# Reordered merge rounds in a hybrid decoder layer: sums and lower parts apart from their casts, weights loaded three units ahead

## The chip, the cores and the metric

The kernel runs on one core of a Trainium2 chip. The core has five engines that run side by side, each through its own list of instructions in a fixed order, and that meet only through semaphores: TensorE (PE in the profile, its weight loads PEld), VectorE (DVE), ScalarE (ACT), GpSimd (POOL) and SyncE (SP), whose list here is mainly the DMA queue that all large loads stand in. The metric is the device time of one execution in microseconds (us), as the median of several runs.

## The reference

One decoder layer over 1024 tokens and a model width of 1024, in float32. A state-space mixer and a latent attention run in parallel from the same projection; this case concerns what joins them.

```python
y_ssd = ssd_mixer(...) @ w_ssd_proj[i]          # (1024 x 2048) @ (2048 x 1024)
y_mla = mla_mixer(...) @ w_mla_proj[i]
g_ssd, g_mla = jnp.split(jax.nn.sigmoid(gates + gate_b[i]), 2, axis=-1)
x = x + (g_ssd * y_ssd + g_mla * y_mla) @ w_o[i]
h = rms_norm(x, norm_ffn_g[i])
u = causal_depthwise_conv(h @ w_up[i], conv_ffn_w[i], conv_ffn_b[i])
u_gate, u_val = jnp.split(u, 2, axis=-1)
x = x + (jax.nn.silu(u_gate) * u_val) @ w_down[i]
```

## The kernel before

Every float32 matmul is done as three matmuls of two-part numbers: an operand is split into a high part, which ScalarE casts (`S.copy`), and a low part, which VectorE (or GpSimd) makes as the operand less its high part; `mm3` multiplies high by high, high by low and low by high. So each operand costs a cast and a subtraction, and the subtraction waits for the cast. `split`, `ordered_split` and `quarter_split` do this (lines L146 and L153 are the casts, L148 and L154 the low parts).

The *merge* is the product of the state-space output with `w_ssd_proj`. It is cut in two along the tokens, along the inner dimension and along the outputs, and the eight products of quarters are got from seven (a Winograd scheme). Products 1 and 2 take quarters as they are; 7, 6, 5, 3 and 4 take sums and differences of activations, of weights or of both. Product p has four tiles of 128 outputs, i = 0 to 3, so there are 28 *units* (p, i), numbered 0 to 27 in the order 1, 2, 7, 6, 5, 3, 4. A unit is eight steps of three 128x128x512 matmuls. Units 0 and 1 are done by `first_products` ahead of the merge; units 2 to 27 are the loop `for n in range(2, len(units))`.

Inside unit n the loop prepares what comes next: it loads the weights of unit n+2 (`weights_raw`), sums and splits those of unit n+1 (`weights`), and sums and splits two tiles of activations for the next product (`acts`), whose raw values were loaded a unit before (`acts_raw`). Weights' sums are kept in `e1`, activations' sums in `sums` (both tiles called `x2` in the trace, or `x`). Each activation goes through sum, cast, low part before the next one starts. After its matmuls, `finish_unit` copies the bank (ScalarE) or adds it (VectorE). In products 3 and 4 the gates come in: `gates` loads two tiles of 256 KB (`gt` from `g_d`, the gate, `mt` from `m_d`, the attention's share), `gated` makes two VectorE operations of them and a finished bank, and `merged` splits the result for the next stage (one ScalarE pass, one VectorE operation).

The weights' high and low parts (`whi`, `wlo`) have two buffers each, `wraw` two, `lt` three. `ur1` and `ur2` are two buffers each of 512 KB.

The *w_o stage* follows: for each half of the tokens and each half of the outputs (`ch`), four steps of 24 matmuls, each with 512 KB of `w_o` loaded into two `wraw` tiles and split, with the remaining gates in between. At the end of four steps the banks are added to the residual `x`, which has been loaded into a tile of 2 MB for each half. In the second half `w_up` is split for the feed-forward stage (`w_raw` loads it into `ur1` and `ur2`).

At the end, the kernel ties the instructions of each engine, SP's DMAs among them, to the order of the program text for the range from `merge` to `merge_end`; outside it TensorE alone is tied throughout, and the other engines are placed by a scheduler, which may set an untied instruction between tied ones.

## Time and profile before

| | |
|---|---|
| median of 3 runs | 2222.56 us (2220.64 to 2222.77) |
| the profiled execution | 2221.28 us, span 2219.5 us |
| TensorE busy | 2136.7 us, 96% of the span |
| VectorE, ScalarE, GpSimd busy | 1501.0, 1074.4, 868.2 us |
| mean granted clock of TensorE | 0.992 |
| the loop of the merge (units 2 to 27) in the trace | from 1266 to 1469.5 us |
| the first half of the w_o stage | from 1469.5 to 1513 us |

Time in a trace is counted from the start of the span. A matmul's busy time overlaps with the next one's, so TensorE's pace is read from starts, not from busy time. In the rows of chains and waits an arrow points back at what was waited for: `PE dps L175 <- ACT whi L153` is TensorE at line 175, which waits for ScalarE's write of `whi` at line 153.

### The profile page before, as it was taken

To read this page: it belongs to the slowest core of one execution; us is meant where nothing else is said; L and a number is where in the kernel's file an instruction comes from. 1 tells how busy PE (TensorE), PEld (TensorE's weight loads), DVE (VectorE), ACT (ScalarE), POOL (GpSimd) and SP (SyncE) were. 2 spreads that over 40 slices of the span, in tenths; PEclk is the share of its full clock that TensorE was granted. 3 is DMA by queue.
4 is the path that set the end of the run, shared out by engine and by line. 5 is a ranking of instruction groups with operands and counts; after the bars stand their busy time and mean duration, and the time that the engine had idled before them with its cause. 6 is when DMAs were issued, how large, how long until landed. Compare 5 with 4: busy or idle time off the path is not lost.

```text
span 2219.5 us, 30213 instructions
## 1 busy us (share of the span) xinstructions
PE 2136.7 (96%) x10748; PEld 1696.6 (76%) x10748; DVE 1501.0 (68%) x2637; ACT 1074.4 (48%) x2044; POOL 868.2 (39%) x969
## 2 busy tenths in 40 slices
PE   8999999999999999999999988699999999999999
PEld 7877777777777887778878765577778888888887
DVE  4466656676673479898877656566886667667873
ACT  5445454545454446565654433234665455554431
POOL 2234433443343246665555200001178777750000
PEclk9999999999999999999999999899999999999999
DMA  4221111111113224545276564665133233338852
GB/s 146 72 64 54 40 48 59 54 40 47 65 44 116 73 95 136 197 143 180 91 249 197 185 209 137 221 202 180 48 114 105 100 109 104 105 136 307 281 192 81
DMA packets 129143, 278.93 MB, mean 126 GB/s; under 512 B 14112, under 2 KB 26336, under 8 KB 128992
## 3 DMA queue, kind: packets, MB, share of 16 engines
q1 hardware_dynamic: 115536, 232.82, 31.3%
q0 software_dynamic: 11968, 40.90, 5.4%
q10 hardware_dynamic: 1488, 3.28, 0.4%
q8 instruction: 84, 1.38, 0.3%
q14 instruction: 67, 0.55, 0.1%
HBM read 210.36 MB, written 66.58 MB: 125 GB/s over the span
## 4 chain that ended last, share of the span: by engine, by line
PE 66%; DVE 17%; ACT 6%; DMA 6%; issue 3%; POOL 1%; SPq 0%; ACTq 0%; DVEq 0%; POOLq 0%
PE lin L175 11%; PE lin L177 11%; PE lin L176 11%; PE dps L177 6%; PE dps L175 6%; PE dps L176 6%; PE pv L694 2%; PE s L175 2%; DVE xg L836 2%; PE s L176 2%; PE s L177 2%; DVE wlo L154 1%; PE s L651 1%; DMA gt<-g_d 1%; ACT whi L153 1%
## 5 line engine op out<-in xcount | busy, mean ns | idle before, releaser
L175 PE MATMUL lin<-h,whi 128*128 128x512 f32 x1248 | 518.0, 415 | 5.9 <-ACT whi L153 3.8
L177 PE MATMUL lin<-h,wlo 128*128 128x512 f32 x1248 | 489.5, 392 | 2.1 <-DVE wlo L154 2.1
L176 PE MATMUL lin<-h,whi 128*128 128x512 f32 x1248 | 488.1, 391 | 0.0
L175 PEld LDWEIGHTS lin<-h,whi 128*128 128x128 f32 x1248 | 234.9, 188 | 82.7 <-issue 33.8
L177 PEld LDWEIGHTS lin<-h,wlo 128*128 128x128 f32 x1248 | 234.4, 188 | 55.9 <-DVE wlo L154 4.0
L176 PEld LDWEIGHTS lin<-h,whi 128*128 128x128 f32 x1248 | 235.6, 189 | 45.8 <-issue 7.0
L154 POOL TENSOR_TENSOR wlo<-wraw,whi 128x512 fp32r<-128x512 f32 x134 | 192.4, 1453 | 173.3 <-ACT whi L153 169.5
L153 ACT CAST whi<-wraw 128x512 fp32r<-128x512 f32 x192 | 116.1, 619 | 173.6 <-PE lin L176 74.1
L688 POOL TENSOR_TENSOR acc<-acc,e 128x512 f32<-128x512 f32 (+3 forms) x80 | 78.8, 985 | 245.2 <-ACT e L683 223.3
L683 ACT ACTIVATE e<-s 128x512 f32<-128x512 f32 (+1 forms) x192 | 93.4, 492 | 152.2 <-DVE s L681 131.1
L175 PE MATMUL dps<-h,whi 128*128 128x512 f32 x244 | 101.1, 414 | 27.9 <-ACT whi L153 27.9
L1163 DVE TENSOR_TENSOR xlo<-ur,xhi 128x512 fp32r<-128x512 f32 (+1 forms) x40 | 82.8, 2071 | 58.6 <-ACT xhi L1162 58.6
L1171 POOL TENSOR_TENSOR us<-ur 128x512 f32<-128x512 f32 x20 | 29.9, 1497 | 203.0 <-DMA ur<-in_w_up 201.6
L177 PE MATMUL dps<-h,wlo 128*128 128x512 f32 x244 | 101.3, 415 | 6.8 <-DVE wlo L154 6.8
L874 ACT ACTIVATE seg<-abc,acum 128x128 f32<-128x128 f32 x256 | 80.2, 389 | 48.8 <-PE yp L915 41.9
L176 PE MATMUL dps<-h,whi 128*128 128x512 f32 x244 | 99.3, 407 | 0.0
L175 PE MATMUL dps<-tq,h 128*128 128x512 f32 x242 | 95.6, 395 | 0.0
L176 PE MATMUL dps<-tq,h 128*128 128x512 f32 x242 | 95.5, 394 | 0.0
L177 PE MATMUL dps<-tq,h 128*128 128x512 f32 x242 | 95.5, 394 | 0.0
L836 DVE SCALAR_TENSOR_TENSOR xg<-craw,cl,xg 128x1024 f32<-128x1024 f32 x48 | 73.7, 1536 | 27.4 <-ACT xg L834 26.9
L175 PEld LDWEIGHTS dps<-h,whi 128*128 128x128 f32 x244 | 48.8, 200 | 43.1 <-ACT whi L153 33.7
L688 DVE TENSOR_TENSOR acc<-acc,e 128x512 f32<-128x512 f32 (+3 forms) x80 | 55.0, 688 | 37.9 <-ACT e L683 37.3
(673 smaller groups left out, 5403.2 us busy)
## 6 DMA issues: line engine op xcount, KB each, us to landing
wraw<-in_w_main SPq DMA_DIRECT2D x112, 256.0 KB
ur<-in_w_up SPq DMA_DIRECT2D x43, 512.0 KB
abc<-ac_d POOLq DMA_DIRECT2D x32, 512.0 KB, 5.2
ar<-f_d SPq DMA_DIRECT2D x32, 512.0 KB
lt<-y_d SPq DMA_DIRECT2D x47, 256.0 KB
g_d<-lt SPq DMA_DIRECT2D x32, 256.0 KB
z_d<-lt SPq DMA_DIRECT2D x32, 256.0 KB
zt<-z_d POOLq DMA_DIRECT2D x32, 256.0 KB, 3.3
```

The source lines that it names most:

```text
L153: S.copy(hi, raw)
L154: (eng or V).tensor_sub(lo, raw, hi.bitcast(F32))
L175: PE.matmul(ps, lhsT=ah, rhs=bh, start=first, stop=False, **more)
L176: PE.matmul(ps, lhsT=ah, rhs=bl, start=False, stop=False, **more)
L177: PE.matmul(ps, lhsT=al, rhs=bh, start=False, stop=last, **more)
L683: S.activation(e[:, c0:512], ps[:, 0:w], AF.Exp)
L688: (V if hd else G).tensor_tensor(accs[hd][:, c0:512], accs[hd][:, c0:512], e[:, c0:512], op=ALU.add)
L694: PE.matmul(pv[hd * 64:(hd + 1) * 64, c0:512], lhsT=vt[:, j, hd * 64:(hd + 1) * 64], rhs=es[hd][:, c0:512], start=first, stop=last)
L836: V.scalar_tensor_tensor(c, raw[:, k:k + T], col(cw + k), c, op0=ALU.mult, op1=ALU.add)
L874: S.activation(seg[:, hd, :], abc[:, hd, :], AF.Relu, bias=acum[:, c, 8 * g + hd:8 * g + hd + 1], scale=-1.0)
L1163: eng.tensor_sub(lo, r, hi.bitcast(F32))
L1171: eng.tensor_tensor(q.s[:, 0:4, :], q.r2[:, 0:4, :], q.r2[:, 4:8, :], op=ALU.add)
```

## The change

It rewrites the merge loop's order and some loads around it.

- `acts` is cut in three: `acts_sum` (VectorE), `acts` (two casts), `acts_low` (two low parts). A unit runs both sums, then both casts, then the close of the unit before, then both low parts.
- `weights` is cut in two: `weights_sum(n + 2)`, and `weights(n + 1)` with cast and low part. `weights_raw` is called for unit n+3 instead of n+2. All units but 2 load their weights into `ur1` and `ur2`; every second activation tile goes to `wraw` instead of `lt`.
- The four tiles of `e1`, loaded at once ahead of the loop before, are loaded one in each of units 2 to 5. `e1` and `sums` change places in memory.
- `finish_unit` of a unit is called in the next one. The gate work of products 3 and 4 (`gate_first`, `gate_second`) now lies wholly within the loop; two of its eight were in the w_o stage.
- Gates' loads are placed by a table (`loads`, `pairs_of`): those of gates 0, 1 and 2 in products 6 and 5, the others one to three units ahead of use.
- The residual of each half is loaded in four pieces of 512 KB, the first half's in units 24 to 27, the second's in the first four steps of w_o. The weights of w_o's first two steps are loaded in units 25 and 27, those of the first step split in unit 27. The loads of `w_up` are tied to stand behind what SP has issued by then.

The core of the diff:

```diff
-            e1, e2 = [ep.tile([P, 4, D], F32, name="x2") for _ in range(2)]
+            e2, e1 = [ep.tile([P, 4, D], F32, name="x2") for _ in range(2)]
             sums = e2.rearrange("p i (k c) -> p (i k) c", c=512)
...
             def weights_raw(n):
                 if n < len(units):
                     p, i = units[n]
-                    if p in plain:
-                        raws[n] = quarter_raw(plain[p][0] + i, plain[p][1])
+                    ct, h = plain.get(p) or other[p]
+                    if n == 2:
+                        raws[n] = quarter_raw(ct + i, h)
                     else:
                         raws[n] = up.tile([P, KD, P], F32, name=f"ur{1 + n % 2}", bufs=2).rearrange(flat)
-                        raw_q(raws[n], other[p][0] + i, other[p][1])
-
-            def weights(n):
+                        raw_q(raws[n], ct + i, h)
+
+            def weights_sum(n):
...
-                    ws[n] = quarter_split(r if p in plain else [r if p < 6 else e])
+
+            def weights(n):
+                if n == len(units):
+                    ws[n] = wo_split(0, 0, wo_first)
+                    wo_first.extend(wo_raw(0, 1))
+                else:
+                    r = raws[n]
+                    ws[n] = quarter_split(r if n == 2 else [e1[:, units[n][1]] if units[n][0] in (7, 6) else r])
 
             def acts_raw(m):
-                if m < len(sources):
+                if 0 <= m < len(sources):
                     p, kk = sources[m]
                     h, half = {7: (0, 1), 6: (1, 1), 5: (0, 0), 3: (1, 0), 4: (1, 1)}[p]
-                    fresh[m] = raw_load(y_d, quarter_k(kk, h), hs_(half), lt.tile([P, 512], F32, name="lt"))
+                    t = wpool.tile([P, 512], F32, name="wraw", bufs=2) if m % 2 else lt.tile([P, 512], F32, name="lt")
+                    fresh[m] = raw_load(y_d, quarter_k(kk, h), hs_(half), t)
                     if p == 7:
                         raw_load(y_d, quarter_k(kk, 0), hs_(0), sums[:, kk])
 
...
-                forms[p].append(ordered_split(r if p > 5 else t))
+            def acts_sum(m):
+                if 0 <= m < len(sources):
...
+
+            def acts(ms):
+                ms = [m for m in ms if 0 <= m < len(sources)]
+                new = []
+                for m in ms:
+                    p, kk = sources[m]
+                    r, t = sums[:, kk] if p > 5 else fresh[m], act_tile()
+                    S.copy(t[:, 0, :], r)
+                    forms[p].append(t)
+                    new.append((r, t))
+                return new
+
+            def acts_low(new):
+                for r, t in new:
+                    V.tensor_sub(t[:, 1, :], r, t[:, 0, :].bitcast(F32))
+
+            def gates_raw(i, one):
+
+                if i not in gm:
+                    if i in (2, 6):
+                        u = up.tile([P, KD, P], F32, name="us", bufs=1).rearrange(flat)
+                        gm[i] = u[:, 0:512], u[:, 512:1024]
+                    else:
+                        gm[i] = [em.tile([P, 512], F32, name=n) for n in ("gt", "mt")]
+                nc.sync.dma_start(out=gm[i][one], in_=(m_d if one else g_d)[i * P:(i + 1) * P, hs_(0)])
...
-            def second_quadrant(i, gm):
-                ml.append(merged(gated(gm, X[i], mr[i]), act_tile()))
-
-            for i in range(2):
-                finish_unit(1, i)
-            weights_raw(2)
+            def gate_first(i):
+                ma.append(merged(gated(gm[i], us[i][:, 0, :], us[i][:, 0, :]),
+                                 em.tile([P, 2, 512], F32R, name="ma", bufs=4)))
+
+            def gate_second(i):
+                ml.append(merged(gated(gm[4 + i], X[i], mr[i]), act_tile()))
...
+            bigs = []
+
+            def x_load(half, i):
+                r0 = half * 512 + i * P
+                nc.sync.dma_start(out=bigs[half][:, i], in_=x[r0:r0 + P, :])
+
+            loads = {(6, 0): (0, 0), (6, 1): (0, 1), (6, 2): (1, 0), (6, 3): (1, 1), (5, 0): (2, 0), (5, 1): (2, 1)}
+            pairs_of = {(3, 1): 3, (3, 2): 4, (3, 3): 6, (4, 0): 5, (4, 2): 7}
+            wo_first = []
+            for n in (2, 3, 4):
+                weights_raw(n)
+            for m in (0, 1):
+                acts_raw(m)
             weights(2)
-            weights_raw(3)
-            for i in range(4):
-                raw_q(e1[:, i], 4 + i, 1)
             for n in range(2, len(units)):
                 p, i = units[n]
+                weights_raw(n + 3)
+                for m in (2 * n - 6, 2 * n - 5):
+                    if m > 1:
+                        acts_raw(m)
+                if n < 6:
+                    raw_q(e1[:, n - 2], 4 + n - 2, 1)
+                if (p, i) in loads:
+                    gates_raw(*loads[p, i])
+                weights_sum(n + 2)
                 weights(n + 1)
-                weights_raw(n + 2)
-                for m in range(2 * n - 8, 2 * n - 6):
-                    if 0 <= m < len(sources):
-                        acts(m)
-                for m in range(2 * n - 6, 2 * n - 4):
-                    if m >= 0:
-                        acts_raw(m)
+                ms = (2 * n - 8, 2 * n - 7)
+                for m in ms:
+                    acts_sum(m)
+                new = acts(ms)
+                if n == 2:
+                    finish_unit(1, 0)
+                    finish_unit(1, 1)
+                else:
+                    finish_unit(*units[n - 1])
+                acts_low(new)
                 if p == 3:
-                    gm[i] = gates(i, 0)
-                elif p == 4 and i < 2:
-                    gm[4 + i] = gates(4 + i, 0)
+                    gate_first(i)
+                elif p == 4:
+                    gate_second(i)
+                if (p, i) in pairs_of:
+                    for one in range(2):
+                        gates_raw(pairs_of[p, i], one)
+                if p == 4:
+                    if i == 0:
+                        bigs.append(ep.tile([P, 4, D], F32, name="x2"))
+                    elif i == 1:
+                        wo_first += wo_raw(0, 0)
+                    x_load(0, i)
...
-                finish_unit(p, i)
-                if p == 4 and i < 2:
-                    second_quadrant(i, gm[4 + i])
+            finish_unit(4, 3)
             merge_end = len(nc.cur_bb.bb.instructions)
-            bigs = [ep.tile([P, 4, D], F32, name="x2") for _ in range(2)]
-            for half in range(2):
-                nc.sync.dma_start(out=bigs[half], in_=x[hs_(half), :].rearrange("(i p) c -> p i c", p=P))
+            bigs.append(ep.tile([P, 4, D], F32, name="x2"))
...
                         if not half:
-                            if ch == 0 and n_ < 2:
-                                second_quadrant(2 + n_, gates(6 + n_, 0))
-                                ms = ma + ml
-                            else:
-                                i = 4 * ch + n_ - 2
-                                if i < 4:
-                                    gated(gates(4 + i, 1), mc[i], mc[i])
+                            i = 4 * ch + n_ - 2
+                            if 0 <= i < 4:
+                                gated(gates(4 + i, 1), mc[i], mc[i])
                             if ch:
                                 gated(gates(n_, 1), us[n_][:, 1, :], mr[n_])
...
+                        if (half, ch, n_) == (0, 0, 0):
+                            wh, wl = ws[len(units)]
+                        else:
+                            wh, wl = wo_split(ch, kp, wo_first[2:] if (half, ch, n_) == (0, 0, 1) else wo_raw(ch, kp))
+                        if not half and not ch:
+                            name = last(mybir.EngineType.SP)
+                            x_load(1, n_)
+                            behind(name)
 
                         if not half and ch and n_ > 1:
                             if n_ == 2:
                                 m22 = []
-                                w_raw(q0)
-                                w_raw(q1)
+                                for q in (q0, q1):
+                                    w_raw(q, last(mybir.EngineType.SP))
```

What moves is shown at three places. First VectorE, in unit 12, the first of product 6, before (the weights' sum and low part of unit 13, then two activations for product 5; `x2_12810` holds the weights' sums here, `x2_12811` the activations'):

```order
L1287 TENSOR_TENSOR x2_12810<-x2_12810,ur2_13259 128x1024
L154 TENSOR_TENSOR wlo_13301<-x2_12810,whi_13300 128x1024
L1308 TENSOR_TENSOR lt_13270<-x2_12811,lt_13270 128x512
L148 TENSOR_TENSOR h_13308<-lt_13270,h_13308 128x512
L1308 TENSOR_TENSOR lt_13272<-x2_12811,lt_13272 128x512
L148 TENSOR_TENSOR h_13312<-lt_13272,h_13312 128x512
```

and in the changed kernel, unit 12 again (`x2_12811` now holds the weights' sums; the first row is the sum of unit 14, the second the low part of unit 13):

```order
L1288 TENSOR_TENSOR x2_12811<-x2_12811,ur1_13243 128x1024
L154 TENSOR_TENSOR wlo_13300<-x2_12811,whi_13299 128x1024
L1318 TENSOR_TENSOR lt_13246<-x2_12810,lt_13246 128x512
L1318 TENSOR_TENSOR wraw_13248<-x2_12810,wraw_13248 128x512
L1335 TENSOR_TENSOR h_13305<-lt_13246,h_13305 128x512
L1335 TENSOR_TENSOR h_13307<-wraw_13248,h_13307 128x512
```

Before, each sum is followed by its own low part; now the weights' sum is one unit ahead of the low part behind it, and the two sums of activations stand ahead of the two low parts.

Second SP's queue at the start of the merge, before (`y_d` is the output of the state-space mixer, `in_w_ssd` the merge's weights):

```order
L988 DMA y_d_75<-xg_10609 128x512 x4
L188 DMA wraw_12836<-in_w_ssd 128x512
L188 DMA wraw_12837<-in_w_ssd 128x512
L1252 DMA x2_12810<-in_w_ssd 128x512 x8
L188 DMA wraw_12854<-in_w_ssd 128x512
L188 DMA wraw_12855<-in_w_ssd 128x512
L188 DMA wraw_12889<-in_w_ssd 128x512
L188 DMA wraw_12890<-in_w_ssd 128x512
L139 DMA lt_12893<-y_d_75 128x512
L139 DMA x2_12811<-y_d_75 128x512
```

and in the changed kernel:

```order
L988 DMA y_d_75<-xg_10609 128x512 x4
L1252 DMA ur2_12828<-in_w_ssd 128x512 x2
L1252 DMA ur1_12831<-in_w_ssd 128x512 x2
L139 DMA lt_12834<-y_d_75 128x512
L139 DMA x2_12810<-y_d_75 128x512
L139 DMA wraw_12837<-y_d_75 128x512
L139 DMA x2_12810<-y_d_75 128x512
L1252 DMA ur2_12846<-in_w_ssd 128x512 x2
L1252 DMA x2_12811<-in_w_ssd 128x512 x2
L1252 DMA ur1_12881<-in_w_ssd 128x512 x2
L1252 DMA x2_12811<-in_w_ssd 128x512 x2
```

The weights of units 3, 4 and 5 (`ur2`, `ur1`, `ur2`) and the first activations move ahead of the tiles of `e1` (here `x2_12811`), which come singly.

Third SP's queue in the second half (`ch` = 1) of the w_o stage's first half of tokens, before, from the weights of the third step (`wraw_14301`) to those of the fourth (`wraw_14355`) and the gates behind:

```order
L1397 DMA wraw_14301<-in_w_o 128x2x256
L1397 DMA wraw_14305<-in_w_o 128x2x256
L1233 DMA gt_14247<-g_d_77 128x512
L1235 DMA mt_14249<-m_d_78 128x512
L1233 DMA gt_14253<-g_d_77 128x512
L1235 DMA mt_14255<-m_d_78 128x512
L1397 DMA wraw_14355<-in_w_o 128x2x256
L1397 DMA wraw_14359<-in_w_o 128x2x256
L1233 DMA gt_14293<-g_d_77 128x512
L1235 DMA mt_14295<-m_d_78 128x512
L1233 DMA gt_14347<-g_d_77 128x512
L1235 DMA mt_14349<-m_d_78 128x512
```

and in the changed kernel, where the weights of the fourth step are `wraw_14330` and `wraw_14332`:

```order
L1235 DMA mt_14226<-m_d_78 128x512
L1233 DMA gt_14230<-g_d_77 128x512
L1235 DMA mt_14232<-m_d_78 128x512
L1149 DMA ur2_14287<-in_w_up 128x1024
L1233 DMA gt_14270<-g_d_77 128x512
L1235 DMA mt_14272<-m_d_78 128x512
L1149 DMA ur1_14290<-in_w_up 128x1024
L1149 DMA ur2_14291<-in_w_up 128x1024
L1233 DMA gt_14324<-g_d_77 128x512
L1235 DMA mt_14326<-m_d_78 128x512
L1373 DMA wraw_14330<-in_w_o 128x2x256
L1373 DMA wraw_14332<-in_w_o 128x2x256
```

The fourth step's weights move behind the last gates, and loads of `w_up` come to stand among those gates: three of four are seen here (`ur2`, `ur1`, `ur2`), the first stands two rows further ahead.

More of the change, by code (lines that the diff above doesn't have):

```diff
@@ L1294, in acts_raw @@
                     p, kk = sources[m]
                     h, half = {7: (0, 1), 6: (1, 1), 5: (0, 0), 3: (1, 0), 4: (1, 1)}[p]
[L1296 removed]
+                    t = wpool.tile([P, 512], F32, name="wraw", bufs=2) if m % 2 else lt.tile([P, 512], F32, name="lt")
+                    fresh[m] = raw_load(y_d, quarter_k(kk, h), hs_(half), t)
                     if p == 7:
                         raw_load(y_d, quarter_k(kk, 0), hs_(0), sums[:, kk])
[L1300 to L1311 removed]
+            def acts_sum(m):
+                if 0 <= m < len(sources):
+                    p, kk = sources[m]
+                    r, t = sums[:, kk], fresh[m]
+                    if p == 7:
+                        V.tensor_tensor(r, r, t, op=ALU.subtract)
+                    elif p == 6:
+                        V.tensor_tensor(r, t, r, op=ALU.subtract)
+                    elif p == 5:
+                        V.tensor_tensor(t, r, t, op=ALU.add)
+                    elif p == 3:
+                        V.tensor_tensor(t, t, r, op=ALU.subtract)
@@ new lines, in gate_second, with wo_raw @@
+            def gate_second(i):
+                ml.append(merged(gated(gm[4 + i], X[i], mr[i]), act_tile()))
+            def wo_raw(ch, kp):
+                raws = []
+                for k in range(2):
+                    n = 2 * kp + k
+                    raw = wpool.tile([P, 512], F32, name="wraw", bufs=2)
+                    nc.sync.dma_start(out=raw.rearrange("p (b c) -> p b c", c=256),
+                                      in_=w_o[2 * ch:2 * ch + 2, n // 4, :, n % 4, :].rearrange("b p c -> p b c"))
+                    raws.append(raw)
+                return raws
@@ new lines, in wo_split @@
+            def wo_split(ch, kp, raws):
+                wh, wl = [wpool.tile([P, 2, 512], F32R, name=n) for n in ("whi", "wlo")]
+                for k, raw in enumerate(raws):
+                    split(raw, wh[:, k, :], wl[:, k, :], w_eng[0])
+                return wh, wl
+            bigs = []
[3 more added lines that the diff above has]
+            loads = {(6, 0): (0, 0), (6, 1): (0, 1), (6, 2): (1, 0), (6, 3): (1, 1), (5, 0): (2, 0), (5, 1): (2, 1)}
```

21 lines of the change are left out of this document (1 added, 20 removed).

## The prediction, made before the changed kernel ran

> **What bounds the kernel now.** I read the page first, then the time by stretches, then who waits for whom, and last the chain of the stretch concerned.
>
> ```profile
> span 2219.5 us, 30213 instructions
> ...
> PE 2136.7 (96%) x10748; PEld 1696.6 (76%) x10748; DVE 1501.0 (68%) x2637; ACT 1074.4 (48%) x2044; POOL 868.2 (39%) x969
> ```
>
> TensorE carries the kernel (the page's first part: busy time, share, instructions). Cut by the merge's stages (the first row is units 2 to 7, the second 8 to 19, the third 20 to 27, the fourth the first half of the w_o stage):
>
> ```profile
> core 0: us, PE busy (x) PEld busy (x) DVE busy (x) ACT busy (x) POOL busy (x), PEclk, DMA share, GB/s
> 1266.00:1306.00 40.00, 35.63 (x146) 27.90 (x145) 18.61 (x29) 13.77 (x23) 0.00 (x0) 0.96 0.75 256
> 1306.00:1396.60 90.60, 74.92 (x288) 54.68 (x289) 61.17 (x77) 30.82 (x44) 0.00 (x0) 0.96 0.41 131
> 1396.60:1469.50 72.90, 52.36 (x193) 39.60 (x192) 42.59 (x59) 19.33 (x31) 5.26 (x3) 0.86 0.67 231
> 1469.50:1513.00 43.50, 43.27 (x191) 35.52 (x190) 28.18 (x45) 17.31 (x33) 0.20 (x2) 1.00 0.60 194
> ```
>
> The w_o row shows what TensorE does when nothing holds it: 192 matmuls in 43.5 us at clock 1.00. The merge's last row needs 72.9 us for as many. Its pace is worked out from single rows of the timeline:
>
> ```profile
> 1265.83 0.39 PE L177 MATMUL lin<-h,wlo 128*128 128x512 f32 x1
> ...
> 1469.51 0.39 PE L175 MATMUL dps<-whi,ma 128*128 128x512 f32 x1
> ...
> 1491.27 0.39 PE L175 MATMUL dps<-whi,ma 128*128 128x512 f32 x1
> ```
>
> From 1469.51 to 1491.27 stand 32 groups of three matmuls: 0.68 us a group, 0.227 a matmul, 5.44 for a unit of eight groups. The first products end at 1265.83 + 0.23 = 1266.06 and w_o begins at 1469.51, so the 26 units of the merge take 203.45 us. At 5.44 they would take 141.4. **62.0 us is all that the merge can give.** By stage the excess is 7.3 us in units 2 to 7 (40.0 less 32.7), 25.3 in units 8 to 19 (90.6 less 65.3) and 29.4 in units 20 to 27 (72.9 less 43.5). Who is waited for, from 1250 to 1530:
>
> ```profile
> PE dps L175 <- ACT whi L153: 27.9, 13, 7.6
> PE dps L177 <- DVE wlo L154: 6.8, 10, 1.6
> ```
>
> (The columns are us in total, times, longest.) The weights' high and low parts come late. The chain of one unit of product 6 says why, each row a start, a duration and what ran:
>
> ```profile
> 1336.59 1.23 DVE wlo L154
> 1337.82 0.61 DVE x L1306
> 1338.45 0.63 ACT h L146
> 1339.11 0.69 DVE h L148
> 1339.80 0.61 DVE x L1306
> 1340.43 0.63 ACT h L146
> 1341.69 1.23 DVE x L1287
> 1343.02 1.05 ACT whi L153
> 1344.10 1.23 DVE wlo L154
> ```
>
> From one low part to the next pass 7.51 us, not 5.44. Neither engine is full (61.17 us of VectorE in twelve units is 5.1 each, ScalarE 2.6): the two hand every sum, cast and low part to and fro, and each idles while the other works. In units 20 to 27 loads of gates add to it, the first of them behind the 2 MB of the residual (a row of SP's queue, then one of the chain):
>
> ```profile
> 1399.86 0.39 SPq L1364 DMA_DIRECT2D x<-in_x  x1
> ...
> 1404.40 8.22 DMA gt<-g_d
> ```
>
> **The change, part by part.** The sum is made from the profiled execution, 2221.28 us (span 2219.5 and 1.8 around it). The median of the runs, 2222.56, lies 1.28 higher.
>
> *Sums apart from casts, low parts behind both casts, units 8 to 19.* No instruction is added. In a unit VectorE now does the weight sum of unit n+2, the low part of n+1, two sums of activations, the close of unit n-1, two low parts. Back to back its 128x512 operations start 0.60 apart:
>
> ```profile
> 1499.06 0.69 DVE L1246 SCALAR_TENSOR_TENSOR gt<-gt,ug 128x512 f32<-128x512 f32 x1
> 1499.66 0.68 DVE L154 TENSOR_TENSOR wlo<-wraw,whi 128x512 fp32r<-128x512 f32 x1
> ```
>
> That is 2 x 1.23 + 4 x 0.60 = 4.9 us, and 5.5 in the few units whose close is VectorE's: 5.44 on average is not exceeded. The first cast of the next unit waits for its weight buffer (two of them), that is for the present unit's start; 1.05 + 1.23 puts the low part 2.3 us into the unit, 3.1 before its use. The cast waits for nothing of VectorE's own unit, because the weight sum is a unit old. Gain 25.3, cost nothing: TensorE's 5.44 covers it, and when that cover is gone VectorE is next.
>
> *Gates.* Their 16 transfers of this stage are issued one to eight units ahead, before on the eve of their use. The gate work adds three VectorE operations and one ScalarE pass to units 20 to 27: units 22 and 23 need 2 x 1.23 + 2 x 0.60 + 3 x 0.60 + 0.64 = 6.1 us, 0.7 over, which the 3.1 us in hand take. Gates 5 and 7 come only a unit ahead, 5.44 + 2.4 = 7.8 us before their sum; if both landed as late as the 8.22 row, 0.8 us would be lost. I take 0, since that row stood behind a residual in one piece, which is now cut. Gain 29.4.
>
> *Weights three units ahead, and the front.* The sum of the bytes up to unit 8 is the same; the start and the order are not:
>
> ```profile
> 1263.54 2.09 DMA y_d<-xg
> ...
> 1270.05 5.17 DMA x<-in_w_ssd
> 1275.28 5.20 DMA wraw<-in_w_ssd
> ...
> 1317.85 2.65 DMA lt<-y_d
> ```
>
> Ten pieces of 256 KB went from 1270.05 to 1280.48. One alone took 2.65, so the other nine took 0.86 each. Before, the first of them stood behind a weight load that waited for VectorE (1270.05); now it waits only for the stores of y_d, landed at 1265.63. Say 1265.9. Piece k lands at 1265.9 + 2.65 + 0.86 (k-1): the 34th (weights of unit 9) at 1296.9, the 38th (activations 6 and 7) at 1300.4, the 40th (weights of unit 10) at 1302.1. Unit 2 starts at 1266.06, its cast no longer behind the two copies of finished banks that waited till 1265.9; unit 8 would start at 1298.7. Unit 9's sum ends at 1298.1, unit 8's low part at 1299.4, with use at 1299.15: 0.3 late. Activations 6 and 7 put the next weight sum and unit 9's low part to 1306.0, with use at 1305.05: 0.9 late. With 0.5 for smaller ones the front keeps 1.7 us of its 7.3. Bounds: 0 and 7.3. Each SP issue behind waits on a buffer freed two units before, so nothing queues behind a stuck one for long.
>
> *Residual in pieces.* Two transfers of 2 MB become eight of 512 KB. SP issues six more; the residual is first used at the end of w_o's first four steps, over 16 us on. Cost 0, hidden by these. [...]
>
> *The end of w_o's first half.* The loads of w_up (2 MB) move from the merge to before the weights of this half's last step, which also stand behind the last gates. The last gate's row before:
>
> ```profile
> 1503.15 0.43 SPq L1235 DMA_DIRECT2D mt<-m_d  x1
> ```
>
> The last step starts 7 x 5.44 = 38.1 us into w_o. Before, its weights were issued ahead of the last gate, whose second transfer went out at 33.6. Now that gate's two transfers go first. Alone the second would land 2.65 later, at 36.3; behind half of w_up's traffic (1 MB, four pieces, 3.4 us) at 39.7, and I take 38.7, since a part will have drained. Then two VectorE operations, a ScalarE pass, the cast and its low part, 0.6 each: 41.7. That is 3.6 us late. Bounds: 0 (w_up lands between other waits) and 8 (all 2 MB in front, 6.9, and one hand-off more). After such a gap the clock drops too:
>
> ```profile
> 1311.00:1314.00 3.00, 1.48 (x7) 0.90 (x5) 1.82 (x3) 1.04 (x1) 0.00 (x0) 1.00 0.60 180
> 1314.00:1317.00 3.00, 2.44 (x7) 1.73 (x8) 2.30 (x3) 0.62 (x1) 0.00 (x0) 0.82 0.07 13
> 1317.00:1320.00 3.00, 3.00 (x10) 2.28 (x10) 2.31 (x4) 0.62 (x1) 0.00 (x0) 0.62 0.88 305
> ```
>
> TensorE is busy 1.48 of the first three us, so it idles 1.5, and the six us behind run at 0.82 and 0.62: 1.7 us lost besides. I add 1.5: 5.1 in all. [...]
>
> *Sum:* 62.0 - 1.7 - 5.1 = 55.2 us. 2221.28 - 55.2 = 2166.1, and with the 1.28 to the median 2167. The stages behind are on TensorE and start earlier by as much.
>
> **Rivals.** *Loads set the pace.* At the rates of the stretch rows rather than of the ten pieces (256 GB/s, 1.02 us a piece; 231 GB/s, 1.13), piece 38 lands 6 us later, of which some 5 reach TensorE, and the 42 pieces of units 20 to 27 (weights 10, activations 6, gates 14, residual 8, w_o 4) need 47.7 us, 4.2 over 43.5; with 3 for the clock 12 us more: 2179. For it: a DMA share of 0.75 in front. Against: 305 GB/s in single stretches, and before SP waited for buffers.
>
> *VectorE sets the pace.* If the hand-offs still leave 0.6 of idling a unit, 26 units at 6.0: 15 us more, 2182. For it: 5.5 of 5.44 is no margin. Against: only a few units have it.
>
> *Slower.* Every second activation now lies in one of two wraw buffers, and SP's queue stands still till one is free, weights and gates behind it. A buffer's round is landing plus 2.3 us (issue 0.45, sum, cast and low part 0.6 each) and serves two units. At 5.44 landings up to 8.6 us are free; from 13.4 us on (a round of 15.7, the present mean of 7.83 a unit) it is slower, by 10 us for each further us over 20 such loads: 14.5 gives 2233. The longest landing quoted is 8.22.
>
> *No gain.* The time is given back later, 2222. The chain behind shows no wait that isn't tied to this stage.
>
> **How the numbers follow.** Forecast 2167 with 0.67; loads 0.17; VectorE 0.08; slower 0.04; no gain 0.04. The forecast's own range is 2160 (nothing lost in front or w_o) to 2176 (front 7.3, w_o 8). The range goes from 2157 (all 62.0 gained, and the 4 us by which I may have misjudged what follows) to 2186, past both rivals. Faster 0.92, the same within 0.2% (what a measurement of this kernel can tell) 0.04, slower 0.04.
>
> **What would show it.** Units 8 to 19 at 5.44 us each, clock 1.00 and few waits of TensorE for whi or wlo; w_o starting near 1409; no gate load in the chain; a wait for whi near 38 us into w_o. I am wrong if units run at 6 us or more, or if the DMA share near 0.9 goes with waits for lt, wraw or ur.

## The result and the profile after

| | before | after |
|---|---|---|
| median of 4 runs | 2222.39 us (2220.64 to 2222.77) | 2168.45 us (2167.05 to 2171.67) |
| ratio, 95% interval | | 0.9761 (0.9744 to 0.9778) |
| the profiled execution | 2221.28 us | 2171.67 us |
| merge, units 2 to 27 | 203.45 us | 143.2 us |
| first half of the w_o stage | 44.05 us | 53.76 us |

The page, as shown of before:

```profile
span 2169.9 us, 30190 instructions
...
PE 2121.0 (98%) x10748; PEld 1694.3 (78%) x10748; DVE 1501.1 (69%) x2628; ACT 1072.6 (49%) x2035; POOL 869.5 (40%) x969
```

VectorE and ScalarE are busy for as long as before (1501 and 1073 us); the span is shorter because TensorE waits less for them and runs less at a low clock (mean granted clock 0.996, 0.992 before). The stretches, with the columns of before: units 2 to 7, 8 to 19, 20 to 27, and the first half of w_o:

```profile
1268.47:1302.90 34.43, 33.23 (x146) 26.89 (x145) 21.27 (x28) 13.14 (x18) 0.00 (x0) 1.00 1.00 350
1302.90:1368.17 65.27, 65.27 (x290) 54.06 (x288) 56.96 (x73) 30.70 (x43) 0.00 (x0) 1.00 0.66 212
1368.17:1411.69 43.52, 43.52 (x194) 36.05 (x192) 38.23 (x52) 16.79 (x25) 0.00 (x0) 1.00 0.66 218
1411.69:1465.45 53.76, 45.92 (x194) 37.21 (x192) 34.12 (x50) 18.88 (x38) 5.18 (x5) 0.94 0.66 228
```

From unit 4 to the end of the merge TensorE is busy without a gap at clock 1.00. That the pace is exact shows in single rows of the timeline (the starts of units 2, 8 and 19, of w_o, of the last of its eight steps and of the second half):

```profile
1268.47 0.39 PE L175 MATMUL dps<-h,whi 128*128 128x512 f32 x1
...
1302.89 0.39 PE L175 MATMUL dps<-h,whi 128*128 128x512 f32 x1
...
1362.73 0.39 PE L175 MATMUL dps<-h,whi 128*128 128x512 f32 x1
...
1411.69 0.39 PE L175 MATMUL dps<-whi,ma 128*128 128x512 f32 x1
...
1457.74 0.80 PE L175 MATMUL dps<-whi,h 128*128 128x512 f32 x1 [7.81 <-ACT whi L153]
...
1465.45 0.39 PE L175 MATMUL dps<-whi,ma 128*128 128x512 f32 x1
```

Units 8 to 18 take 59.84 us, 5.44 each; w_o starts 8 x 5.44 + 65.27 behind unit 8. What is left to wait for from 1250 to 1480:

```profile
PE dps L175 <- ACT whi L153: 8.5, 2, 7.8
PE dps L176 <- DVE wlo L154: 0.7, 1, 0.7
PE dps L177 <- DVE wlo L154: 0.5, 1, 0.5
```

Of 34.7 us (27.9 + 6.8) remain 9.7, and 7.8 of them are one wait, ahead of w_o's last step. Its chain (start, duration, what ran):

```profile
1437.62 6.65 DMA gt<-g_d
...
1447.86 7.22 DMA gt<-g_d
...
1457.09 0.61 ACT whi L153
...
1457.74 0.80 PE dps L175
```

In the kernel before, the second half of w_o starts at

```profile
1513.56 0.39 PE L175 MATMUL dps<-whi,ma 128*128 128x512 f32 x1
```

so its first half took 44.05 us by its starts, not 43.5: its last step was 0.5 us late. The profiled executions then differ by 60.2 us gained in the merge, 9.7 lost in w_o's first half, 1.5 gained behind it (705.9 us against 704.5 from the second half on) and 2.4 lost ahead of the merge, where nothing was changed: 49.6. In the traces of the twelve experiments below, which all share that part, the merge starts anywhere from 1261.2 to 1266.8, so those 2.4 are taken for scatter.

### The profile page after: what moved, and what is told of

Same layout as the page of the kernel before. It is cut to its first block, busy times and chain, and to the rows that moved or that the text cites. A ratio compares the mean times of both kernels' runs of the same rounds, so it can differ in the third digit from the quotient of the medians.

```text
span 2169.9 us, 30190 instructions
## 1 busy us (share of the span) xinstructions
PE 2121.0 (98%) x10748; PEld 1694.3 (78%) x10748; DVE 1501.1 (69%) x2628; ACT 1072.6 (49%) x2035; POOL 869.5 (40%) x969
## 3 DMA queue, kind: packets, MB, share of 16 engines
q8 instruction: 84, 1.38, 0.3%
## 4 chain that ended last, share of the span: by engine, by line
PE 72%; DVE 14%; ACT 5%; DMA 5%; issue 2%; POOL 1%; SPq 0%; ACTq 0%; DVEq 0%; POOLq 0%
PE lin L175 12%; PE lin L177 12%; PE lin L176 12%; PE dps L176 7%; PE dps L175 7%; PE dps L177 7%; PE pv L694 3%; PE s L175 2%; PE s L176 2%; PE s L177 2%; DVE xg L836 1%; PE s L651 1%; PE yp L915 1%; PE s L634 1%; PE sn L898 1%
## 5 line engine op out<-in xcount | busy, mean ns | idle before, releaser
L153 ACT CAST whi<-wraw 128x512 fp32r<-128x512 f32 x174 | 105.7, 618 | 161.4 <-PE lin L176 74.0
L1163 DVE TENSOR_TENSOR xlo<-ur,xhi 128x512 fp32r<-128x512 f32 (+1 forms) x40 | 83.1, 2077 | 58.6 <-ACT xhi L1162 58.6
L175 PE MATMUL dps<-h,whi 128*128 128x512 f32 x244 | 95.0, 390 | 0.7 <-ACT whi L153 0.7
L177 PE MATMUL dps<-h,wlo 128*128 128x512 f32 x244 | 95.2, 390 | 0.5 <-DVE wlo L154 0.5
L176 PE MATMUL dps<-h,whi 128*128 128x512 f32 x244 | 94.9, 389 | 0.0
L694 PE MATMUL pv<-e,vt 128*64 128x512 f32 (+3 forms) x384 | 74.4, 507 | 0.0
```

Of the source, the lines that this page charges most:

```text
L153: S.copy(hi, raw)
L175: PE.matmul(ps, lhsT=ah, rhs=bh, start=first, stop=False, **more)
L176: PE.matmul(ps, lhsT=ah, rhs=bl, start=False, stop=False, **more)
L177: PE.matmul(ps, lhsT=al, rhs=bh, start=False, stop=last, **more)
L694: PE.matmul(pv[hd * 64:(hd + 1) * 64, c0:512], lhsT=vt[:, j, hd * 64:(hd + 1) * 64], rhs=es[hd][:, c0:512], start=first, stop=last)
L1163: eng.tensor_sub(lo, r, hi.bitcast(F32))
```

## The experiments

*Hand-offs* stands for the theory that the separation of sums, casts and low parts made the merge faster, *traffic* for the theory that the 2 MB of `w_up` between the last gates made w_o slower. The before kernel ran beside each group, with medians of 2218.62, 2221.3 and 2221.88 us, so ratios are compared. Merge and w_o (its first half) are stretches of each trace, from first matmul to first matmul.

| run | median us | ratio (95%) | merge | w_o |
|---|---|---|---|---|
| the change | 2168.45 | 0.9761 (0.9744 to 0.9778) | 143.2 | 53.8 |
| old_order | 2203.06 | 0.9931 (0.9914 to 0.9947) | 176.4 | 55.0 |
| wsum_late | 2184.83 | 0.9836 (0.9818 to 0.9855) | 158.4 | 54.9 |
| acts_chain | 2181.13 | 0.9815 (0.9798 to 0.9832) | 156.0 | 54.1 |
| lows_twice | 2186.95 | 0.9850 (0.9836 to 0.9863) | 159.6 | 54.4 |
| two_ahead | 2171.64 | 0.9789 (0.9774 to 0.9803) | 148.1 | 52.7 |
| gates_eve | 2166.57 | 0.9758 (0.9745 to 0.9772) | 143.2 | 53.4 |
| res_whole | 2167.85 | 0.9767 (0.9751 to 0.9782) | 142.5 | 54.6 |
| gates_behind_res | 2173.72 | 0.9788 (0.9768 to 0.9808) | 148.7 | 54.7 |
| sums_held | 2168.34 | 0.9773 (0.9758 to 0.9788) | 142.3 | 54.3 |
| wup_late | 2163.65 | 0.9753 (0.9739 to 0.9768) | 142.6 | 44.4 |
| wup_pieces | 2158.87 | 0.9724 (0.9711 to 0.9737) | 142.7 | 44.8 |
| wup_behind | 2159.15 | 0.9722 (0.9705 to 0.9738) | 142.8 | 44.2 |

### The order put back (old_order)

```diff
-                weights_sum(n + 2)
+                weights_sum(n + 1)
                 weights(n + 1)
...
+                new = []
                 for m in ms:
                     acts_sum(m)
-                new = acts(ms)
+                    acts_low(acts([m]))
```

> Weights' sum back beside its own cast, each activation's sum, cast and low part back in a chain; all loads, gates and the residual stay as changed. Theory (hand-offs): VectorE idles again 1.05 us for the weights' cast and twice 0.69 for the activations', 4.84 + 2.4 = 7.3 us a unit against 5.44, in the 20 units that prepare activations: 37 us more, 2205 (2195 to 2210). Rival (the earlier loads are what made it faster): the units stay at 5.44 to 5.7, 2168 to 2174.

The merge is 33.2 us longer, as the hand-offs want it. Units 8 to 18, first in this run and then in the kernel before, by stretch:

```profile
1299.06:1383.10 84.04, 67.14 (x265) 49.03 (x263) 55.30 (x70) 27.57 (x38) 0.00 (x0) 0.98 0.47 151
```

```profile
1305.92:1390.22 84.30, 69.14 (x265) 50.23 (x265) 56.25 (x70) 28.05 (x39) 0.00 (x0) 0.96 0.43 136
```

84.04 us and 84.30: with the old order and all the new loads, these units are as slow as before the change. VectorE's waits in the same stretch (us, times, longest), again this run and then before:

```profile
DVE h L1335 <- ACT h L1328: 15.1, 22, 0.7
DVE wlo L154 <- ACT whi L153: 14.9, 12, 1.5
```

```profile
DVE h L148 <- ACT h L146: 15.1, 22, 0.7
DVE wlo L154 <- ACT whi L153: 14.1, 12, 1.2
```

It is the same idling, 0.69 us for each activation's cast and 1.2 for the weights'. So in this stage nothing of the gain is left without the new order, whatever the new loads do. The new order with the old loads was not run, and the later close of a unit was not put back.

### One hand-off at a time (wsum_late, acts_chain)

Each has one of the two hunks above.

> Only the weights' sum back beside its own cast; activations as changed. Theory (each hand-off costs VectorE its idle time, and TensorE what goes beyond 5.44): 1.05 us more in the units whose weights are summed (13 of the 20 that prepare activations, products 6, 5 and 4): 4.84 + 1.05 = 5.9, 0.45 over, 6 to 9 us more, 2174 to 2178. Rival (one hand-off a unit hides in what is in hand): 2168 to 2170.

> Only the activations back in their chain of sum, cast, low part; the weights' sum as changed. Theory: VectorE idles twice 0.69 a unit, 4.84 + 1.38 = 6.2, 0.78 over in 20 units: 16 us more, 2184 (2180 to 2190); with the run of the weights' sum alone it falls short of the 37 us of both together, since 0.6 us a unit is in hand once only. Rival (the activations' hand-offs are what counts, all of it): 35 us, 2203.

`acts_chain` is at 6.23 us a unit, as expected, and 12.8 us longer in the merge than the change. `wsum_late` misses its expectation: 15.2 us longer, 9 expected at most. In units 8 to 21 it loses 8.6 us, within the 6 to 9 that were expected; the other 7 come in units 22 to 27, at 5.9 to 7.5 us, where the gates' operations fill VectorE. The expectation had left these operations out. Its waits from 1312.4 to 1407, and those of `acts_chain` from 1304.6 to 1368:

```profile
DVE wlo L154 <- ACT whi L153: 15.4, 14, 1.5
```

```profile
DVE h L1335 <- ACT h L1328: 13.7, 20, 0.7
```

Apart they cost 12.8 and 15.2, together 33.2: what VectorE has in hand in a unit is given away only once.

### VectorE's margin (lows_twice)

```diff
-                for r, t in new:
+                for r, t in new + new:
                     V.tensor_sub(t[:, 1, :], r, t[:, 0, :].bitcast(F32))
```

> Each activation's low part is made twice, with the same result: two more VectorE operations of 0.60 in the 20 units that prepare activations. Theory (VectorE is next behind TensorE, 4.84 us of 5.44 a unit): 6.04 a unit, 0.6 over, 20 x 0.6 = 12 us more less what is in hand, 2176 to 2182, with waits of TensorE for whi and wlo. Rival (TensorE waits for nothing of VectorE's, the handing over leaves room): within 2 us of 2168. A second rival (VectorE was the bound already, at 5.44): 24 us more, 2192.

Eight units from the middle of this run:

```profile
1317.37:1365.86 48.49, 45.94 (x194) 35.42 (x192) 46.72 (x64) 19.80 (x29) 0.00 (x0) 1.00 0.60 188
```

6.06 us each, with VectorE busy 46.72 of 48.49: it sets the pace, at the 6.04 that were expected. The total misses its expectation, 16.4 us in the merge and not 12, and that comes again from units with gates (6.4 to 7.6 us in units 20 to 25). In the changed kernel itself VectorE is busy 56.96 / 12 = 4.75 us a unit in units 8 to 19, and 6.06 less the two added operations of 0.60 is 4.86, so 0.6 to 0.7 us a unit is all that stands between TensorE's pace and VectorE's.

### Weights two units ahead (two_ahead)

```diff
-            for n in (2, 3, 4):
+            for n in (2, 3):
                 weights_raw(n)
...
-                weights_raw(n + 3)
+                weights_raw(n + 2)
```

> Weights loaded two units ahead in SP's queue instead of three; all else as changed. Theory (hand-offs): SP runs up to a unit ahead of the engines and is held by buffers, landings of 2.65 to 4.4 us fit; a few stalls in front, 2168 to 2172. Rival (the third unit of lead is what made it faster): the weights' sum waits for its load in every unit, 1 to 2 us each, 26 to 50 us more, 2195 to 2220.

Units 8 to 24 stay at 5.44: SP's queue, held by buffers and not by the loop, is early enough. The 5.0 us are lost in units 25 and 26. Unit 27's weights now stand behind a gate's two tiles and a piece of the residual, VectorE waits 3.2 us to sum them, and unit 26's low part is next in VectorE's list (two rows of the chain):

```profile
1390.75 7.22 DMA ur<-in_w_ssd
...
1399.56 1.22 DVE wlo L154
```

Neither theory had that place. The third unit of lead is needed where the queue is fullest, at the end.

### Gates and residual (gates_eve, res_whole, gates_behind_res)

```diff
-                if (p, i) in loads:
-                    gates_raw(*loads[p, i])
+                if p in (3, 4):
+                    for one in range(2):
+                        gates_raw(i if p == 3 else 4 + i, one)
...
-                if (p, i) in pairs_of:
-                    for one in range(2):
-                        gates_raw(pairs_of[p, i], one)
```

> Both loads of each of gates 0 to 7 back to the start of the unit that uses them; all else as changed, the residual in pieces. Theory: SP runs up to a unit ahead of the engines, a pair lands 2.7 to 4.4 us after its issue, so with no 2 MB transfer ahead most come in time: 0 to 6 us more, 2168 to 2174. Rival (the lead of the gates' loads carried what the hand-offs did not, 29.4 less 8 x 2.07): 13 us more, 2181.

```diff
-                r0 = half * 512 + i * P
-                nc.sync.dma_start(out=bigs[half][:, i], in_=x[r0:r0 + P, :])
+                if i == 0:
+                    nc.sync.dma_start(out=bigs[half], in_=x[hs_(half), :].rearrange("(i p) c -> p i c", p=P))
...
-                            behind(name)
+                            if n_ == 0:
+                                behind(name)
```

> The residual of each half in one transfer of 2 MB, issued where the first of its four pieces was; all else as changed. Theory (bytes count, not transfers; but what stands behind 2 MB waits 6.9 us longer): gates 5, 6 and 7 and w_o's first weights, which have 5.4 to 11 us of lead, come 0 to 8 us late: 2168 to 2178. [...]

Both change nothing that can be measured (ratios 0.9758 and 0.9767 against 0.9761). The gates' early loads were not needed, and six transfers more or fewer are not seen either. Then both old features at once, the residual ahead of gate 0:

```diff
+                if (p, i) == (3, 0):
+                    bigs.append(ep.tile([P, 4, D], F32, name="x2"))
+                    nc.sync.dma_start(out=bigs[0], in_=x[hs_(0), :].rearrange("(i p) c -> p i c", p=P))
+                if p in (3, 4):
+                    for one in range(2):
+                        gates_raw(i if p == 3 else 4 + i, one)
...
-                    x_load(0, i)
```

> Both put back at once: gates 0 to 7 loaded at the start of the unit that uses them, and the first half's residual in one piece of 2 MB ahead of gate 0, as before the change. Each alone had cost nothing (gates late: ratio 0.9758; residual whole but behind the first gates: 0.9767). Theory (it is the 2 MB ahead of the gates that made them late): gate 0 lands some 7 us later, VectorE waits 3 to 6 us, of which 3.1 are in hand: 1 to 6 us more, 2169 to 2174. Rival 1 (they carried the part of 29.4 us that the hand-offs do not, 29.4 less 8 x 2.07): 13 us more, 2181. Rival 2 (SP's lead hides it all): 2168.

VectorE's wait for gates in the last units of this run (from 1349 to 1411), and the row of TensorE that follows from it:

```profile
DVE gt L1246 <- DMA gt<-g_d: 6.0, 1, 6.0
```

```profile
1373.99 0.80 PE L175 MATMUL dps<-h,whi 128*128 128x512 f32 x1 [2.99 <-ACT whi L153]
```

6.0 us of VectorE's become 3.0 of TensorE's, so the 3.1 us in hand are there; but the low clock behind the gap adds 3.4 (units 19 to 22 take 6.4 us too much by their starts). In the kernel before, the same wait stood at

```profile
DVE gt L1246 <- DMA gt<-g_d: 21.4, 5, 8.5
```

in units 19 to 27, and these units were 20.7 us slower than in `old_order` (79.3 us against 58.6): TensorE waited 21.0 us there instead of 7.1, and most of the rest is low clock (0.72 granted from 1409 to 1446). Only the first of the five waits, 8.5 us, is for a gate whose load was issued behind the first residual. The next two, 6.0 and 5.3 us, have another reason, which the chain of before shows (`SPq` is an issue by SP):

```profile
1412.65 0.70 DVE gt L1246
...
1416.58 1.30 DVE h L148 x2
1417.88 0.10 SPq L139
...
1418.02 5.78 DMA gt<-g_d
```

VectorE waits for a gate, then makes the low parts that free the buffers for which SP's queue stands still, and only then is the next gate's load issued, which is VectorE's next wait. In `gates_eve` and `gates_behind_res` SP is ahead of that circle, and only gate 0 is waited for by more than 0.5 us (0.8 and 6.0). That the new order and buffers broke it is read from these traces and not shown by a run: old order, old buffers, late gates and early residual were not put back together short of the kernel before, which also loads `w_up` there.

### The wait in w_o (sums_held, wup_late, wup_pieces, wup_behind)

The trace of the change has a second suspect: beside the w_up loads, GpSimd's sums of them. Three VectorE rows of the change, then the three GpSimd rows beside them:

```profile
1448.19 1.78 DVE L1241 SCALAR_TENSOR_TENSOR mu<-mr,mu 128x512 fp32r<-128x512 f32 x1
1449.89 1.74 DVE L1246 SCALAR_TENSOR_TENSOR gt<-gt,mu 128x512 f32<-128x512 f32 x1
1451.67 1.63 DVE L1247 TENSOR_TENSOR mr<-gt,mt 128x512 f32<-128x512 f32 x1
```

```profile
1447.64 1.78 POOL L1171 TENSOR_TENSOR us<-ur 128x512 f32<-128x512 f32 x1 [4.96 <-DMA ur<-in_w_up]
...
1449.50 1.59 POOL L1172 TENSOR_TENSOR us<-us,ur 128x512 f32<-128x512 f32 x1
1451.05 1.71 POOL L1177 TENSOR_TENSOR ur<-ur,ur 128x512 f32<-128x512 f32 x1
```

`sums_held` makes GpSimd wait, by a small sum that reads the last bank's result first:

```diff
+                            done = x2b[0][:, 3, D - 4:D]
...
+                            G.tensor_tensor(t[:, 0, 0:4], done, done, op=ALU.add)
-                            w_sums(q, act_tile().rearrange("p a (b c) -> p (a b) c", c=P).bitcast(F32) if n_ else None)
+                            w_sums(q, t)
```

> The loads of w_up stay where the change put them; only GpSimd's sums of them are held till the last bank of w_o's first half is done. In the changed kernel three VectorE operations beside these sums took 1.6 to 1.8 us instead of 0.69. Theory (traffic): they go back to 0.69, but the last gate still lands as late, so the wait stays at 7 to 8 us and the time at 2168, within 2 us. Rival (the slowed VectorE is what is late): the wait shrinks by the 3.2 us that the three operations lose, 2165 or less, with less idle time and so less low clock behind it.

```profile
1443.64 0.69 DVE L1246 SCALAR_TENSOR_TENSOR gt<-gt,mu 128x512 f32<-128x512 f32 x1
...
1448.75 0.69 DVE L1246 SCALAR_TENSOR_TENSOR gt<-gt,mu 128x512 f32<-128x512 f32 x1 [1.80 <-DMA gt<-g_d]
```

The operations are back at 0.69, VectorE idles instead for the last gate, and w_o takes 54.3 us: the slowing is real and costs nothing here. The other three move the loads of `w_up`. `wup_late` sends all of them in the first two steps of the second half:

```diff
-                                for q in (q0, q1):
-                                    w_raw(q, last(mybir.EngineType.SP))
...
+                        if half and not ch and n_ < 2:
+                            w_raw(pairs[n_], last(mybir.EngineType.SP))
```

> Theory (traffic): the wait of 8.0 us ahead of the last step of w_o's first half, and the 2.3 us at a low clock behind it, come from the 2 MB of w_up that stand between the last gates in SP's queue. Moved to the start of the second half they have over 20 us until their first use and need about 6.9 us (8 x 0.86), so both go and nothing takes their place: 2168 - 10 = 2158 us. Rival 1: the last gates alone are late, since their buffers come free late: 3 to 4 us of wait stay, 2162 to 2164. Rival 2: the 2 MB now delay the second half's own weights of w_o, and the stall only moves: 2166 to 2170.

The first half is at 44.4 us, so the theory holds for the wait; but the second rival comes true in part. The second half's third step waits:

```profile
PE dps L175 <- ACT whi L153: 3.1, 1, 3.1
```

with a low clock behind it (matmuls 0.43 us apart from 1469.9 to 1473.7, 0.23 from 1474 on), and from the second half on the run takes 710.9 us instead of 704.5: 6.4 of the 9.4 are lost again, and the ratio's interval overlaps with the change's. `wup_pieces` sends one 512 KB piece behind the weights of each of steps 2 to 5:

```diff
+                        if half and 0 < 4 * ch + n_ < 5:
+                            q, r = pairs[(4 * ch + n_ - 1) // 2], (4 * ch + n_ - 1) % 2
+                            t = up.tile([P, KD, P], F32, name=f"ur{1 + r}", bufs=2)
...
+                            nc.sync.dma_start(out=t, in_=w_up[r * FFT + q.j])
```

> The loads of w_up one piece of 512 KB at a time, behind the weights of the second half's steps 2, 3, 4 and 5 (before the moved kernel sent all 2 MB ahead of step 3's weights, which then came 3.1 us late, with a low clock behind). Theory (traffic): each piece adds 1.7 us to a queue that has 5.44 us a step, so neither the first half's last step nor the second half's third one waits by more than 1 us: 10 us under the changed kernel, ratio to before 0.9715, about 2158. Rival (the 2 MB store of the first half's result, not w_up, held the third step's weights): the 3.1 us stay and the time is that of the run with w_up moved in one go, ratio 0.975.

2158.87 us, 0.9724 (0.9711 to 0.9737) against the change's 0.9761 (0.9744 to 0.9778): the fastest version along with the next, about 8 us below the change. The second half's third step still waits 1.4 us, where the theory had 1 at most. From 1400 to 1530 TensorE waits for

```profile
PE dps L1206 <- DVE x L279: 3.6, 1, 3.6
PE dps L175 <- ACT whi L153: 1.4, 1, 1.4
PE dps L176 <- DVE wlo L154: 0.9, 2, 0.6
```

`wup_behind` sends the same pieces behind the weights of steps 3, 4, 4 and 5:

```diff
-                        if half and 0 < 4 * ch + n_ < 5:
...
+                            for k in {2: (0,), 3: (1, 2), 4: (3,)}.get(4 * ch + n_, ()):
```

> As the run with w_up in pieces of 512 KB, each a step later (behind the second half's weights of steps 3, 4, 4 and 5), so that none stands ahead of the 2 MB store of the first half's result and of the third step's weights. Theory (bytes ahead in the queue): these come 1.7 us earlier, so the third step's wait of 1.4 us goes, and the norm that waits for the store (3.6 us ahead of the transposes) gives back 1.7: 2156, ratio 0.971. Rival (the store alone is what they wait for): as the run in pieces, 2159, 0.9724.

```profile
PE dps L176 <- DVE wlo L154: 2.9, 4, 1.4
PE dps L1206 <- DVE x L279: 1.9, 1, 1.9
```

The wait of 1.4 for whi goes and the norm gives back 1.7 (3.6 to 1.9), as the theory says; but the low parts of the weights behind wait 2.0 more, and the time is the rival's. Between these two runs the delay moved and did not go.

## Why the prediction was right, and where it was not

The time came out 1.5 us above the forecast of 2167. The merge's time was forecast rightly; that the whole came so near is in part luck, since one term was half as large as it should have been and others, not forecast, made up for it.

- *Pace, 62.0 us at most.* Right to the hundredth: 5.44 us a unit from unit 4 on, clock 1.00. The row read for it, 43.5 us for w_o's first half before, was cut half a us short of the stage (44.05), which leaves the pace as it is.
- *Units 8 to 19, gain 25.3.* Right in size and cause: 65.27 us against a floor of 65.3, and with the order put back the old time to 0.3 us. The working that VectorE is at 4.9 to 5.5 us a unit and next behind TensorE holds too: 4.75 by its busy time, and with 1.2 more it sets the pace (`lows_twice`).
- *Gates, gain 29.4.* Right in size (43.52 us for units 20 to 27, TensorE's pace, which any cure of the waits would reach), wrong in what the step named. The leads of the gates' loads are not what carried it: without them the time is the same. About a third went with the hand-offs (units 19 to 27 of `old_order` are 9.6 us above the change, those of before 30.3). The rest, by the traces, went with the 2 MB ahead of gate 0 and with the circle of VectorE and SP's queue shown above; how much with each stays open.
- *Front, 1.7 us kept of its 7.3.* 1.8 measured, but in another place, so the number was luck. Units 8 and 9 were not late: the pieces of 256 KB followed one another faster than the 0.86 us taken from before (from 1278 to 1300 the DMA engines moved 386 GB/s, 0.68 us a piece). Units 2 and 3 were, by 0.8 and 0.95: the weights of unit 3, now behind the stores of `y_d`, took 4.35 us, more than the 2.65 assumed. (The working has the use of unit 9's low part at 1305.05; by its own steps it is 1304.9, and the sum would be 0.2 us larger.)

```profile
1269.04 4.35 DMA ur<-in_w_ssd
```

- *Residual in pieces, cost 0.* Right. `res_whole`, with six transfers fewer, took 2167.85 us, the change 2168.45: six transfers more cost nothing that is measured.
- *The end of w_o's first half, cost 5.1.* This term was mis-sized: 10.2 above eight steps of 5.44. The place and the mechanism were right, the step that failed is "behind half of w_up's traffic". The last gate's first transfer landed at 1455.08, 43.4 us into w_o, where the forecast had the gate at 38.7. It was issued late and landed slowly. A gate ahead of it, behind the first piece of `w_up`, took 6.65 us; SP's queue then stood still till VectorE had used that gate and freed a buffer (4.7 us, the shorter of the two waits in the row below, of SP's waits from 1268 to 1470), so the last gate was issued 36.2 us into w_o, behind two more pieces, and took 7.22. The forecast had its second transfer issued at 33.6. The upper bound of 8 was the right value for the wait (7.97 late), and the clock took 2.27, not 1.5.

```profile
SPq L1233 <- DVE ug L1247: 9.7, 2, 5.0
```

- *What made up for it:* 1.5 us behind the half (its third step of the second half takes 6.4 us instead of 9.1) and the 0.5 that before lost in the half, both at 0 in the forecast. By these stages the change gains 52.0 us; the medians differ by 53.9, and the 1.9 between are put down to scatter.
- *Signs.* Units at 5.44, few waits and the place of the last wait came as named. "No gate load in the chain" did not: two stand in it, in w_o.
- *Rivals.* Loads did not set the pace from unit 4 on, though DMA engines were busy 1.00 of units 2 to 7 at 350 GB/s: a full queue is not a late one. VectorE did not, by 0.6 to 0.7 us a unit. SP's queue behind the `wraw` buffers cost nothing in the change; in `two_ahead` a crowded queue cost 5 us, at the end of the merge.

## What to carry to other kernels

Two engines that pass small pieces to and fro idle in turn, and neither looks full (in units 8 to 19 before, VectorE was busy for 5.1 and ScalarE for 2.6 of 7.55 us a unit): add up busy time and waits of both over one unit of work before a load is blamed. Put the sums of all pieces first, then all casts, then all low parts, with the first operand a unit old: here VectorE's waits for casts in units 8 to 18 went from 29.2 us to 3.9 without an instruction more. And ask of each bulk transfer what small, late-needed one stands behind it in its queue: here 2 MB among the last gates cost 10 us in one stage. From the start of w_o to the end the kernel before takes 750.0 us, the change 758.2, and the run with the 2 MB in four pieces behind weights 752.1.

## What the runs showed of the hardware

- *Some gaps in TensorE cost its clock besides.* After a gap of 7.81 us the clock is at half for some 4 us (the change, first two rows), after one of 2.99 us for 6 us (`gates_behind_res`, from 1374 to 1380.3, the next two), and after one of 1.38 us not at all (`wup_pieces`, the last):

```profile
1457.74:1459.74 2.00, 1.98 (x4) 1.28 (x5) 1.37 (x3) 0.47 (x1) 0.00 (x0) 0.50 0.04 11
1459.74:1461.74 2.00, 2.00 (x7) 1.54 (x6) 0.64 (x1) 0.35 (x1) 0.00 (x0) 0.50 0.77 251
```

```profile
1377.00:1379.00 2.00, 2.00 (x6) 1.52 (x6) 1.27 (x2) 1.24 (x2) 0.00 (x0) 0.50 0.77 250
1379.00:1381.00 2.00, 2.00 (x8) 1.58 (x7) 2.00 (x3) 1.36 (x3) 0.00 (x0) 0.67 0.81 177
```

```profile
1463.90:1466.00 2.10, 1.80 (x7) 1.27 (x8) 1.35 (x3) 0.60 (x1) 0.78 (x1) 1.00 0.12 16
```

The price is 2.3 us behind the gap of 7.81 and 3.4 behind that of 2.99, so the gap of 3 us cost 6.4 in all; in `two_ahead` a gap of 2.55 us was followed by 3.5 us of matmuls 0.43 us apart instead of 0.23, which cost 1.8 more. In the kernel before, a gap of 1.55 us that ends at 1314.03, with one of 0.53 that ends at 1315.29, was followed by a clock of 0.50 from 1316 to 1319. Which gaps cost the clock, and which do not, these runs do not settle.

- *VectorE's operations took longer beside GpSimd's.* Its 128x512 operations with two inputs took 1.63 to 1.78 us beside GpSimd's sums, and 0.69 with these held (`sums_held`). Each of the three VectorE rows above ends 0.5 us after the end of a GpSimd row (1449.97 after 1449.42, 1451.63 after 1451.09, 1453.30 after 1452.76). What ties these ends together was not shown.
